# Norms and rope of queries and keys by pairs of heads inside the attention, and the context's attention in two halves behind it

## The chip, the core and the metric

The kernel runs on one core of one Trainium2 chip. The core has five engines that run at the same time and meet only at semaphores: TensorE (PE, matrix products and transposes by the identity), VectorE (DVE), ScalarE (ACT), GpSimd (POOL) and SyncE (SP, which issues transfers). The metric is the device time of one execution in microseconds.

## What is computed

One inference step of a trunk of two layers. Each layer has three mixers side by side (a state-space scan A, an attention B, a gated mixing C), one output projection, and a convolutional feed-forward. 512 latent tokens and 128 context tokens go through it together. The change touches B alone:

```python
def mla_queries(c_q, p, rope):
    q = (rmsnorm(c_q, p['q_a_norm']) @ p['w_uq']).reshape(bn, L, MLA_HEADS, MLA_QK)
    q = rmsnorm(q, p['q_norm'])            # per head, 96 channels
    if rope is not None:                   # latent tokens only
        q = concatenate([q[..., :64], apply_rope(q[..., 64:], *rope)])
    return q

# keys: 64 channels from the compressed kv, 32 shared rope channels, the same norm and rope
# latent queries see 128 cached context keys and the 512 latent keys;
# context queries see the 128 context keys alone, without rope
def one_block(q_blk):
    s = jnp.einsum('bqhd,bkhd->bhqk', q_blk, k).astype(F32) * ATTN_SCALE
    w = jax.nn.softmax(s, axis=-1).astype(v.dtype)
    return jnp.einsum('bhqk,bkhd->bqhd', w, v)
```

There are eight heads of 96 channels, with values of 64. All is in 32-bit floats.

## The kernel before

**Products.** Large products are made of two-part operands (a high part and the rest), each as three matmuls; the score product of one head and one key tile is such a three (`s`, L1267 to L1269). Small ones and transposes (L147) run on plain 32-bit operands.

**What sets the order.** The kernel is written in Tile with a scheduler that simulates the engines in time and gives each engine its own order. The written order is a wish: an instruction stands on its engine where the scheduler put it, and each engine then works strictly in that order. Buffers come from pools with a number of copies per name; a tile that is asked for waits until the oldest copy is free.

**The modulation as filler.** Each layer needs eight blocks of a product with w_mod, in 32 loads of 512 KB. A generator (`fill`) issues one load on SP's queue (L257) and its two matmuls (`mod`, L261) at each call; after a block come a copy on ScalarE (`modev`, L267), four transposes (`modt`) and a small reduce and add on VectorE (L240, L245). The loads have three buffers (`raw`). The calls are strewn over the projections and the attention, and what is left runs out at the end of the attention.

**Norms, before.** The query projection leaves `qs` (128 tokens of a tile on the partitions, 5 tiles, 8 heads, 96 channels; tile 4 is the context), the key projection `ks` (6 tiles: the cached ones and the latents, tile 5 the context). ScalarE squares each tile as it comes (`hsq`, L1061), VectorE sums the squares of each head (`ms`, L1062). `head_scales` turns sums into reciprocal roots in a chain of small operations on VectorE (L102 to L111, L1151 to L1157). `key_norms` writes the rope channels of all keys in one operation (L1163) and scales the others tile by tile (L1166). `query_norms` runs twice: for tile 4 alone, so that the context can start, and then for the four latent tiles: four scalings (L1174) and a rope of six operations over all heads (L1184 to L1189).

**Attention, before.** It begins with the context's: transposes of all eight heads (`ctr`), raw scores for the maxima (`cmx`, L1313), maxima of each query (`nm`, L1314), their transposition into extra rows of the queries (`nmt`, L1319), scores (`cs`, L1328), the exponentials (`Pc`, L1330) and weighted sums with row sums (`co`, L1341 and L1343). In between stand `turn` and `maxima` of heads 0 and 1. `turn(h)` transposes one head's queries and keys (`qt`, `kt`) and splits them into parts (`qh`, `ql`, `kh`, `kl`); `maxima(h)` makes raw scores in halves (`mx`, L1248) and reduces them (`nml`, L1250), with one call of `fill` at each of its four steps; `max_row(h)` transposes the negated maxima into row 96 of `qh` (`nmt`). Then a loop over four pairs of heads: `scores` of both heads (ten P tiles of 128x512, exponentials on ScalarE, L1271), `weighted` (VectorE sums of the P tiles, weighted sums `o`, L1287), and `turn`, `maxima` and `max_row` of the next pair's heads. Behind pairs 1 and 3 four heads are divided by their sums and squared for the norm ahead of the output projection (`wo`).

## Time and profile before

| | us |
|---|---|
| time, median of 3 runs | 1830.92 (1827.31 to 1836.54) |
| the profiled execution | 1831.83 |
| its span, first to last instruction | 1830.0 |
| TensorE busy | 1708.6 (93%) |
| VectorE busy | 1158.5 (63%) |
| ScalarE busy | 681.7 (37%) |
| GpSimd busy | 311.4 (17%) |
| TensorE clock granted, mean | 0.961 of full speed |

Layer 0's attention lies at about 241 to 382 us of the span, layer 1's at 1118 to 1265. The profile lists for each engine its busy time and the instructions in any window; for each wait what ended it; and for each instruction its start and length. PEclk is the share of full speed that TensorE's clock was granted in the window; full speed is 2.4 GHz. Matmuls overlap in the pipeline, so the distance between two starts tells their cost, not one's length. A plain 32-bit matmul leaves two records in the trace (the eight of `cmx` are listed as x16).

### The profile page before, as it was taken

Reading aid. Unit: us, or ns where it says so; the run is one execution under the profiler, and the core shown is the slowest. Engines: PE = TensorE matmul, PEld = TensorE weight load, DVE = VectorE, ACT = ScalarE, POOL = GpSimd, SP = SyncE. Lnnn points to the kernel's source line nnn. Section 1 sums busy time; section 2 is a strip of 40 time slices with the busy share of each in tenths; the row PEclk is TensorE's granted clock in tenths of the full one; section 3 lists DMA queues with packets and bytes.
Section 4 is the critical chain, followed back from the end, with each engine's and each line's share of the span. In section 5 each row is a group of like instructions: output and inputs, shape, how many; then the busy total and the mean of one; then the engine's idle time right before and its main releaser. Section 6 shows DMA issues by size and latency. Waiting matters only on the chain.

```text
span 1830.0 us, 28203 instructions
## 1 busy us (share of the span) xinstructions
PE 1708.6 (93%) x10864; PEld 1499.7 (82%) x10864; DVE 1158.5 (63%) x2421; ACT 681.7 (37%) x1210; POOL 311.4 (17%) x738
## 2 busy tenths in 40 slices
PE   6869789998999999999999888999989999999998
PEld 2668644478889999999999785445989999999998
DVE  6887875667664546456566668475786464555554
ACT  4334444433442424224244355353344232332241
POOL 2886200000195060540000210000000000000000
PEclk8989799999999999999999888999989999999999
DMA  9265453301453523223122633430222131221221
GB/s 297 70 177 152 113 166 122 105 24 47 129 160 111 152 55 117 76 81 110 47 78 79 169 87 121 157 127 1 70 70 93 35 104 47 92 89 39 81 82 58
DMA packets 192998, 182.44 MB, mean 100 GB/s; under 512 B 33438, under 2 KB 153052, under 8 KB 192864
## 3 DMA queue, kind: packets, MB, share of 16 engines
q1 hardware_dynamic: 170160, 154.33, 27.5%
q0 software_dynamic: 8272, 23.87, 4.4%
q10 hardware_dynamic: 14432, 2.44, 0.7%
q8 instruction: 86, 1.41, 0.3%
q14 instruction: 48, 0.39, 0.1%
HBM read 161.94 MB, written 18.64 MB: 99 GB/s over the span
## 4 chain that ended last, share of the span: by engine, by line
PE 75%; DVE 10%; DMA 8%; ACT 4%; issue 2%; POOL 1%; ACTq 1%; DVEq 0%; POOLq 0%
PE up L141 11%; PE up L143 11%; PE up L142 10%; PE dn L142 5%; PE dn L143 5%; PE dn L141 5%; PE mod L261 3%; DMA raw<-w_mod 3%; PE o L1287 3%; PE wo L141 1%; PE wo L143 1%; PE wo L142 1%; DVE wlo L118 1%; DMA raw<-ffn_w_up 1%; PE s L1267 1%
## 5 line engine op out<-in xcount | busy, mean ns | idle before, releaser
L141 PE MATMUL up<-hh,whi 128*128 128x322 f32 x1408 | 436.8, 315 | 9.8 <-ACT hh L357 8.9
L142 PE MATMUL up<-hl,whi 128*128 128x322 f32 x1408 | 439.2, 313 | 1.8 <-DVE hl L358 1.8
L143 PE MATMUL up<-hh,wlo 128*128 128x322 f32 x1408 | 439.8, 314 | 0.0
L141 PEld LDWEIGHTS up<-hh,whi 128*128 128x128 f32 x1408 | 266.1, 190 | 21.8 <-issue 10.8
L142 PEld LDWEIGHTS up<-hl,whi 128*128 128x128 f32 x1408 | 268.3, 191 | 2.7 <-DVE hl L358 2.7
L143 PEld LDWEIGHTS up<-hh,wlo 128*128 128x128 f32 x1408 | 267.3, 190 | 1.0 <-issue 1.0
L118 DVE TENSOR_TENSOR wlo<-raw,whi 128x1024 fp32r<-128x1024 f32 (+1 forms) x116 | 147.4, 1272 | 155.2 <-ACT whi L117 146.5
L142 PE MATMUL dn<-glo,dh 128*128 128x322 f32 (+1 forms) x704 | 217.7, 311 | 0.0
L143 PE MATMUL dn<-gh,dl 128*128 128x322 f32 (+1 forms) x704 | 217.4, 310 | 0.0
L141 PE MATMUL dn<-gh,dh 128*128 128x322 f32 (+1 forms) x704 | 208.9, 310 | 2.3 <-DVE xT L1501 1.5
L1501 DVE SCALAR_TENSOR_TENSOR xT<-dn,mod,xT 128x320 f32<-128x320 f32 (+2 forms) x288 | 112.1, 435 | 128.2 <-PE dn L143 128.1
L117 ACT CAST whi<-raw 128x1024 fp32r<-128x1024 f32 (+1 forms) x116 | 120.6, 1041 | 157.1 <-PE up L142 63.8
L1532 ACT ACTIVATE cv<-up,prm,cw 128x321 f32<-128x321 f32 x88 | 54.1, 619 | 259.0 <-PE up L143 255.0
L143 PEld LDWEIGHTS dn<-gh,dl 128*128 128x128 f32 x704 | 132.9, 189 | 0.0
L141 PEld LDWEIGHTS dn<-gh,dh 128*128 128x128 f32 x704 | 130.4, 189 | 2.8 <-DVE xT L1501 1.8
L142 PEld LDWEIGHTS dn<-glo,dh 128*128 128x128 f32 x704 | 132.7, 188 | 0.0
L261 PE MATMUL mod<-raw,sT 128*32 128x512 f32 x384 | 89.7, 642 | 21.7 <-DMA raw<-w_mod 19.8
L1533 DVE SCALAR_TENSOR_TENSOR cv<-up,cw,cv 128x320 f32<-128x320 f32 x88 | 48.3, 549 | 74.3 <-ACT cv L1532 74.1
L118 DVE TENSOR_TENSOR dl<-raw,dh 128x1024 fp32r<-128x1024 f32 x44 | 53.9, 1224 | 38.3 <-ACT dh L117 38.2
L1250 DVE TENSOR_REDUCE nml<-mx 128x1 f32<-128x640 f32 x64 | 51.1, 819 | 28.3 <-PE mx L1248 28.2
L117 ACT CAST dh<-raw 128x1024 fp32r<-128x1024 f32 x44 | 46.1, 1048 | 50.7 <-DMA raw<-ffn_w_down 44.5
L141 PE MATMUL wo<-yh,whi 128*128 128x322 f32 (+1 forms) x192 | 60.0, 318 | 1.7 <-ACT yh L117 0.9
(472 smaller groups left out, 3367.4 us busy)
## 6 DMA issues: line engine op xcount, KB each, us to landing
raw<-w_mod SPq DMA_DIRECT2D x96, 512.0 KB, 4.3
raw<-ffn_w_up SPq DMA_DIRECT2D x88, 512.0 KB, 3.9
raw<-ffn_w_down SPq DMA_DIRECT2D x44, 512.0 KB, 3.4
raw<-w_in SPq DMA_DIRECT2D x10, 512.0 KB, 5.0
we<-WEd POOLq DMA_DIRECT2D x8, 512.0 KB, 4.4
qt<-Qd POOLq DMA_DIRECT2D x8, 512.0 KB, 5.0
raw<-w_out SPq DMA_DIRECT2D x16, 256.0 KB, 4.8
raw<-w_out SPq DMA_DIRECT2D x8, 512.0 KB, 3.4
```

Source lines behind the costliest of these rows:

```text
L117: self.nc.scalar.copy(hi, raw)
L118: self.nc.vector.tensor_tensor(lo, raw, hi.bitcast(F32), op=OP.subtract)
L141: mm(ps, wh, xh, start=start, stop=False)
L142: mm(ps, wh, xl, start=False, stop=False)
L143: mm(ps, wl, xh, start=False, stop=stop)
L261: nc.tensor.matmul(ps[c:c + 32, :], self.sT[:, k, :], rv[:, j, :], start=k < 4, stop=k >= 4)
L1250: V.tensor_reduce(nm[:, tt:tt + 1], pb[:, :, :320], axis=AX.XY, op=OP.max, negate=True)
L1267: mm(ps, kh[i][:, kc_], qh[i], start=True, stop=False)
L1287: mm(pb[i * 64:(i + 1) * 64, 0], Vt[:, kt, 2 * p + i], Ps[i][kt], start=kt == 0, stop=kt == 4)
L1501: self.nc.vector.scalar_tensor_tensor(self.xT[:, m, a:b], po[:, a - lo:b - lo], self.modcol(l, gi, m, c), self.xT[:, m, a:b], op0=OP.mult, ...
L1532: A.activation(z[:, 0:321], po[:, 0:321], AF.Identity, bias=b, scale=c1)
L1533: V.scalar_tensor_tensor(z[:, 1:321], po[:, 0:320], c0, z[:, 1:321], op0=OP.mult, op1=OP.add)
```

## The change

Queries and keys keep their raw projections until the attention. The reciprocal roots are made ahead of it for all tiles at once, one chain of 40 columns for the queries and one of 48 for the keys. `prepare(p)` then scales and ropes the two heads of pair p: four kinds of operations over all tiles of these heads, and a rope of six. The written order puts `prepare(p + 1)` behind the scores of pair p's first head. `ready(h)` is `turn`, `maxima` with `fill`, and `max_row` of one head; the first two heads' stand ahead of the loop, a later pair's first head behind the first scores of the pair before, and its second behind the weighted sums. The context's attention goes from the front into the loop: `context(0)` (four heads) behind pair 1 and `context(1)` behind pair 2, each with its own transposes, maxima, scores and sums, its tiles out of the ten P buffers (three for each half), and its one-hot rows loaded anew in each half.

```diff
-        self.key_norms(pt, ks, sc, ms, krn, kg)
+        RK, RsK = self.head_scales(pt, keep, ms, sc, 5, 6, krn)
...
-            if tt == 4:
-                self.query_norms(l, pt, qs, sc, ms, tab, [4])
-        self.query_norms(l, pt, qs, sc, ms, tab, [0, 1, 2, 3])
+        RsQ, = self.head_scales(pt, keep, ms, sc, 0, 5)
...
+        def prepare(p):
+            hs = slice(2 * p, 2 * p + 2)
+            V.tensor_tensor(ks[:, :, hs, 0:64], ks[:, :, hs, 0:64],
+                            bc(RsK[:, :, hs, None], [128, 6, 2, 64]), op=OP.mult)
+            V.tensor_tensor(ks[:, :, hs, 64:96], bc(kg[:, :, None, :], [128, 6, 2, 32]),
+                            bc(RK[:, :, hs, None], [128, 6, 2, 32]), op=OP.mult)
+            V.tensor_tensor(qs[:, :, hs, :], qs[:, :, hs, :],
+                            bc(RsQ[:, :, hs, None], [128, 5, 2, 96]), op=OP.mult)
+            V.tensor_tensor(qs[:, 4, hs, 64:96], qs[:, 4, hs, 64:96],
+                            bc(self.qgr[l][:, None, :], [128, 2, 32]), op=OP.mult)
+            x1, x2 = qs[:, 0:4, hs, 64:80], qs[:, 0:4, hs, 80:96]
+            sh = [128, 4, 2, 16]
+            x = [at.tile(sh, F32, name=self.uid("qx"), tag=f"qx{i}") for i in range(4)]
+            tb = [bc(tab[:, i][:, :, None, :], sh) for i in range(4)]
+            for i, y in enumerate((x1, x2, x2, x1)):
+                V.tensor_tensor(x[i], y, tb[i], op=OP.mult)
+            V.tensor_tensor(x1, x[0], x[1], op=OP.subtract)
+            V.tensor_tensor(x2, x[2], x[3], op=OP.add)
...
+        def context(b):
+
+            qc, kc, Pc = (t("P", [128, 512], bufs=10).rearrange("p (h c) -> p h c", h=4)
+                          for _ in range(3))
...
+            A.copy(qc[96:100], bc(ps[:4, None, :128], [4, 4, 128]))
...
+        def ready(h):
+            turn(h)
+            for _ in maxima(h):
+                next(fill, None)
+            max_row(h)
+
+        prepare(0)
+        ready(0)
+        ready(1)
         merge_ac_stats()
         for p in range(4):
...
-            heads = (2 * p + 2, 2 * p + 3) if p < 3 else ()
-            out = weighted(p, [scores(2 * p), scores(2 * p + 1)])
-            for h in heads:
-                turn(h)
+            Ps = [scores(2 * p)]
+            if p < 3:
+                prepare(p + 1)
+                ready(2 * p + 2)
+            Ps.append(scores(2 * p + 1))
+            out = weighted(p, Ps)
             next(out)
-            for h in heads:
-                for _ in maxima(h):
-                    next(fill, None)
+            if p < 3:
+                ready(2 * p + 3)
             next(out)
-            for h in heads:
-                max_row(h)
+            if p in (1, 2):
+                context(p - 1)
```

How the scheduler's order changes is seen at three places. On TensorE in layer 1, right behind the query projection and two blocks of the modulation, there stood before:

```order
L147 MATMUL kt_11603<-ident,ks_11224 96x128 x5
L147 MATMUL kt_11633<-ident,ks_11224 96x128 x5
L147 MATMUL ctr_11572<-ident,qs_11223 96x128 x4
L147 MATMUL ctr_11578<-ident,qs_11223 96x128 x4
L147 MATMUL ctr_11584<-ident,ks_11224 96x128 x4
L147 MATMUL ctr_11590<-ident,ks_11224 96x128 x4
L1313 MATMUL cmx_11614<-kc_11570,qc_11569 128x128 x4
L1313 MATMUL cmx_11620<-kc_11570,qc_11569 128x128 x4
L147 MATMUL nmt_11643<-ident,nm_11613 8x128
L1328 MATMUL cs_11690<-qc_11569,kc_11570 128x128 x4
L1328 MATMUL cs_11697<-qc_11569,kc_11570 128x128 x4
L147 MATMUL qt_11596<-ident,qs_11223 96x128 x4
```

and stands now:

```order
L147 MATMUL kt_11560<-ident,ks_11237 96x128 x5
L147 MATMUL qt_11553<-ident,qs_11236 96x128 x4
L261 MATMUL mod_11601<-raw_11602,sT 32x512 x2
L261 MATMUL mod_11601<-raw_11642,sT 32x512 x2
L261 MATMUL mod_11601<-raw_11650,sT 32x512 x2
L1250 MATMUL mx_11571<-kh_1761_11527,qh_1757_11523 128x320 x2
L1250 MATMUL mx_11579<-kh_1761_11527,qh_1757_11523 128x320 x2
L147 MATMUL modt_11606<-ident,modev_11595 128x128 x4
L261 MATMUL mod_11601<-raw_11658,sT 32x512 x2
L1250 MATMUL mx_11587<-kh_1761_11527,qh_1757_11523 128x320 x2
L147 MATMUL nmt_11614<-ident,nml_11570 1x128
L1250 MATMUL mx_11597<-kh_1761_11527,qh_1757_11523 128x320 x2
```

The context's transposes, maxima and scores (`ctr`, `cmx`, `nmt`, `cs`) are gone from between the first head's keys and queries, only head 0 is transposed before the first maxima, and three loads' `mod` matmuls stand between.

On VectorE in layer 1, from the latent tiles' reciprocal roots (`Rs`) to the last step of the rope, there stood before:

```order
L1157 TENSOR_TENSOR Rs_1738_11494<-rs_y_1737_11484,sc_10013 128x32
L1174 TENSOR_TENSOR qs_11223<-qs_11223,Rs_1738_11494 128x768 x4
L1314 TENSOR_REDUCE nm_11613<-cmx_11614 128x4
L1314 TENSOR_REDUCE nm_11613<-cmx_11620 128x4
L1184 TENSOR_TENSOR qx_11500<-qs_11223,qtab_11243 128x512
L1185 TENSOR_TENSOR qx_11501<-qs_11223,qtab_11243 128x512
L1186 TENSOR_TENSOR qx_11502<-qs_11223,qtab_11243 128x512
L1187 TENSOR_TENSOR qx_11503<-qs_11223,qtab_11243 128x512
L1188 TENSOR_TENSOR qs_11223<-qx_11500,qx_11501 128x32x16
L1189 TENSOR_TENSOR qs_11223<-qx_11502,qx_11503 128x32x16
```

Now there stand, from the roots of all five tiles to the first operation of the second pair's rope:

```order
L1165 TENSOR_TENSOR Rs_1744_11479<-rs_y_1743_11469,sc_10026 128x40
L1178 TENSOR_TENSOR qs_11236<-qs_11236,Rs_1744_11479 128x5x192 x4
L1180 TENSOR_TENSOR qs_11236<-qs_11236,q_normr_1991 128x2x32
L1187 TENSOR_TENSOR qx_11543<-qs_11236,qtab_11256 128x128
L1187 TENSOR_TENSOR qx_11544<-qs_11236,qtab_11256 128x128
L1187 TENSOR_TENSOR qx_11545<-qs_11236,qtab_11256 128x128
L1187 TENSOR_TENSOR qx_11546<-qs_11236,qtab_11256 128x128
L1180 TENSOR_TENSOR qs_11236<-qs_11236,q_normr_1991 128x2x32 x3
L1188 TENSOR_TENSOR qs_11236<-qx_11543,qx_11544 128x4x2x16
L1189 TENSOR_TENSOR qs_11236<-qx_11545,qx_11546 128x4x2x16
L1187 TENSOR_TENSOR qx_11754<-qs_11236,qtab_11256 128x128
L1187 TENSOR_TENSOR qx_11755<-qs_11236,qtab_11256 128x128
```

and from the last product of the third pair's rope on, to the first maxima:

```order
L1187 TENSOR_TENSOR qx_11991<-qs_11236,qtab_11256 128x128
L1232 SCALAR_TENSOR_TENSOR ql_1759_11525<-qt_11553,qg_1983,qh_1757_11523 96x512
L1188 TENSOR_TENSOR qs_11236<-qx_11988,qx_11989 128x4x2x16
L1189 TENSOR_TENSOR qs_11236<-qx_11990,qx_11991 128x4x2x16
L1187 TENSOR_TENSOR qx_12288<-qs_11236,qtab_11256 128x128
L1187 TENSOR_TENSOR qx_12289<-qs_11236,qtab_11256 128x128
L1187 TENSOR_TENSOR qx_12290<-qs_11236,qtab_11256 128x128
L1187 TENSOR_TENSOR qx_12291<-qs_11236,qtab_11256 128x128
L1188 TENSOR_TENSOR qs_11236<-qx_12288,qx_12289 128x4x2x16
L1189 TENSOR_TENSOR qs_11236<-qx_12290,qx_12291 128x4x2x16
L1252 TENSOR_REDUCE nml_11570<-mx_11571 128x1
```

All four pairs' scalings (x4) stand together ahead of the first rope, and all four ropes ahead of the first maxima (L1252); nothing of `prepare(1)` to `prepare(3)` stands behind the first scores. Layer 0 has the ropes of pairs 1 to 3 among the first head's four maxima.

On ScalarE in layer 0, around the end of the second pair, there stood before (`yB` and `S` are the weighted sums and row sums of a pair, `P` the exponentials):

```order
L1229 ACTIVATE qh_489_2950<-qt_3303,qg_333 96x512
L1208 COPY yB_2944<-o_3330 128x512
L1211 COPY S_2948<-o_3330 64x512
L267 COPY modev_3410<-mod_3372 128x512
L267 COPY modev_3586<-mod_3416 128x512
L1259 CAST qh_488_2949<-nmt_3434 1x512
L1271 ACTIVATE P_3450<-s_3446 128x512
L1271 ACTIVATE P_3456<-s_3452 128x512
L1271 ACTIVATE P_3462<-s_3458 128x512
L1236 ACTIVATE kh_492_2953<-kt_3513,kg_336 96x512
```

and stand now, with the first half of the context (`P_3572` and `P_3573` are its queries and keys, `P_3574` its exponentials, `whi` the high part of a w_out weight):

```order
L1309 ACTIVATE P_3573<-ctr_3582,kg_336 96x512
L1238 ACTIVATE kh_484_2912<-kt_3508,kg_336 96x128
L267 COPY modev_3724<-mod_3549 128x512
L117 CAST whi_3939<-raw_3938 128x1024
L117 CAST whi_4167<-raw_4166 128x1024
L1318 COPY P_3572<-cnmt_3595 4x512
L1322 ACTIVATE P_3574<-cs_3598 128x512
L1273 ACTIVATE P_3642<-s_3638 128x512
L1273 ACTIVATE P_3648<-s_3644 128x512
L1273 ACTIVATE P_3654<-s_3650 128x512
```

Two casts of w_out weights now stand ahead of the copy of the context's maxima, and behind it stand the exponentials of the context and of the next head.

## Rows read from the trace of the kernel before

**Rows 1.** Page, busy us, share of span, instructions of one engine
```profile
PE 1708.6 (93%) x10864; PEld 1499.7 (82%) x10864; DVE 1158.5 (63%) x2421; ACT 681.7 (37%) x1210; POOL 311.4 (17%) x738
```

**Rows 2.** Windows of A and B: span, busy us by engine, PEclk, DMA share, GB/s
```profile
241.30:275.30 34.00, 29.59 (x171) 13.94 (x170) 21.79 (x40) 14.34 (x29) 3.27 (x6) 0.95 0.71 231
275.30:382.30 107.00, 100.71 (x473) 51.73 (x471) 68.13 (x122) 50.31 (x98) 0.24 (x2) 0.97 0.30 95
1118.30:1156.10 37.80, 29.19 (x154) 17.98 (x152) 24.88 (x52) 14.54 (x28) 0.00 (x0) 0.82 0.34 110
1156.10:1264.90 108.80, 102.24 (x473) 51.90 (x470) 68.23 (x122) 50.63 (x97) 0.24 (x2) 0.97 0.30 97
```

**Rows 3.** Waits of TensorE, 1118 to 1156 us: for whom, total, times, longest
```profile
PE nmt L147 <- DVE nm L1314: 2.1, 1, 2.1
PE ctr L147 <- DVE qs L1177: 1.6, 1, 1.6
```

**Rows 4.** Windows inside layer 1's A, the same columns
```profile
1127.00:1133.00 6.00, 2.77 (x18) 2.28 (x17) 6.00 (x9) 1.49 (x3) 0.00 (x0) 0.78 0.01 3
1133.00:1140.00 7.00, 7.00 (x38) 5.78 (x40) 4.48 (x9) 4.99 (x9) 0.00 (x0) 0.63 0.00 0
...
1148.00:1156.10 8.10, 8.10 (x49) 3.45 (x47) 2.05 (x4) 1.94 (x7) 0.00 (x0) 0.97 0.49 151
```

**Rows 5.** Waits of TensorE, 241 to 276 us
```profile
PE mod L261 <- DMA raw<-w_mod: 4.2, 4, 3.2
```

**Rows 6.** DMA issues, 241 to 276 us: count, KB each, median to landing
```profile
raw<-w_mod SPq DMA_DIRECT2D x15, 512.0 KB, 4.9
```

**Rows 7.** Timeline of VectorE, layer 1: start, us, line, operation, count
```profile
1122.50 0.41 DVE L1177 TENSOR_TENSOR qs<-qs,q_normr 128x256 f32<-128x256 f32 x1
1122.83 0.18 DVE L1151 TENSOR_TENSOR ms<-ms,sc 128x32 f32<-128x32 f32 x1
...
1126.39 0.19 DVE L1157 TENSOR_TENSOR Rs<-rs_y,sc 128x32 f32<-128x32 f32 x1
1126.62 3.56 DVE L1174 TENSOR_TENSOR qs<-qs,Rs 128x768 f32<-128x768 f32 x4
...
1131.30 0.68 DVE L1184 TENSOR_TENSOR qx<-qs,qtab 128x512 f32<-128x512 f32 x1
1131.89 0.68 DVE L1185 TENSOR_TENSOR qx<-qs,qtab 128x512 f32<-128x512 f32 x1
...
1134.42 0.68 DVE L1189 TENSOR_TENSOR qs<-qx,qx 128x512 f32<-128x512 f32 x1
```

**Rows 8.** Groups of TensorE, 241.3 to 282 us: busy us, mean ns
```profile
L1313 PE MATMUL cmx<-kc,qc 96*128 96x128 f32 x16 | 2.2, 281 | 0.0
L1328 PE MATMUL cs<-qc,kc 104*128 104x128 f32 x16 | 1.9, 275 | 0.0
...
L147 PE MATMUL ctr<-ident,ks 128*96 128x128 f32 x8 | 1.2, 278 | 0.0
```

**Rows 9.** Timeline of TensorE before layer 1's first score
```profile
1149.49 0.43 PE L1341 MATMUL co<-Pc,Vt 128*64 128x128 f32 x2
1149.85 0.41 PE L1343 MATMUL co<-Pc,ones 128*32 128x128 f32 x2
1150.19 0.43 PE L1341 MATMUL co<-Pc,Vt 128*64 128x128 f32 x2
```

**Rows 10.** Waits of TensorE, 276 to 383 us
```profile
PE mod L261 <- DMA raw<-w_mod: 3.2, 2, 2.2
...
PE mx L1248 <- DVE nml L1250: 0.5, 1, 0.5
```

**Rows 11.** Waits of TensorE, 1156 to 1265 us
```profile
PE mod L261 <- DMA raw<-w_mod: 3.6, 2, 1.9
PE mx L1248 <- DVE nml L1250: 0.8, 2, 0.5
```

**Rows 12.** Window inside layer 0's B, columns as in the windows above
```profile
335.00:342.00 7.00, 6.75 (x24) 4.39 (x21) 5.42 (x7) 3.74 (x5) 0.00 (x0) 0.58 0.66 218
```

More of the change, by code (lines that the diff above doesn't have):

```diff
@@ L1191, in attention @@
-    def attention(self, l, M, yb, at, es, qs, ks, Vt, yB, yA, yc, ssc, fill):
+        def prepare(p):
[16 more added lines that the diff above has]
+            V.tensor_tensor(x2, x[2], x[3], op=OP.add)
@@ L1194, in attention @@
+        return prepare
+    def attention(self, l, M, yb, at, prepare, qs, ks, Vt, yB, yA, yc, ssc, fill):
         nc, V, A = self.nc, self.nc.vector, self.nc.scalar
@@ L1347, in attention @@
-        at2 = es.enter_context(self.tc.tile_pool(name=f"at2{l}", bufs=1, side=self.sides[1]))
+        def context(b):
+            qc, kc, Pc = (t("P", [128, 512], bufs=10).rearrange("p (h c) -> p h c", h=4)
+                          for _ in range(3))
+            hs = slice(4 * b, 4 * b + 4)
+            nc.sync.dma_start(out=kc[96:100].rearrange("p h c -> p (h c)"),
+                              in_=self.I["k_onehot"][hs, b * 512:(b + 1) * 512])
+            for src, dst, g in ((qs[:, 4], qc, qg), (ks[:, 5], kc, kg)):
+                ps = self.pa("ctr")
+                for i in range(4):
+                    self.tr(ps[:96, i * 128:(i + 1) * 128], src[:, 4 * b + i, :])
+                A.activation(dst[:96].rearrange("p h c -> p (h c)"), ps[:96], AF.Copy, scale=g)
+            nm = t("cnm", [128, 4], bufs=2)
+            ps = self.pa("cmx")
+            for i in range(4):
+                mm(ps[:, i * 128:(i + 1) * 128], qc[:96, i], kc[:96, i], start=True, stop=True)
+            V.tensor_reduce(nm, ps.rearrange("p (h c) -> p h c", h=4), axis=AX.X, op=OP.max,
+                            negate=True)
+            ps = self.pa("cnmt")
+            self.tr(ps[:4, :128], nm)
+            A.copy(qc[96:100], bc(ps[:4, None, :128], [4, 4, 128]))
+            ps = self.pa("cs")
+            for i in range(4):
+                mm(ps[:, i * 128:(i + 1) * 128], kc[:100, i], qc[:100, i], start=True, stop=True)
+            A.activation(Pc.rearrange("p h c -> p (h c)"), ps, AF.Exp, scale=SCALE)
+            for p in range(2 * b, 2 * b + 2):
+                po = self.pb("co")
+                for i in range(2):
+                    Ph = Pc[:, (2 * p + i) % 4]
+                    mm(po[i * 64:(i + 1) * 64, 0, :128], Vt[:, 5, 2 * p + i], Ph,
+                       start=True, stop=True)
+                    r = (2 * p + i) % 4 * 32
+                    mm(po[r:r + 32, 1, :128], self.ones[:, :32], Ph, start=True, stop=True)
+                put(p, po[:, 0], po[:, 1], 128, CX)
+            V.reciprocal(S[:, b, 512:640], S[:, b, 512:640])
```

105 lines of the change are left out of this document (19 added, 86 removed).

## The prediction

> **What bounds the kernel now.** The busy shares of the page say that TensorE is the bound nearly everywhere (93% of the span) [rows 1]. The change touches only the attention of the two layers, so the reader should look at four stretches [rows 2]. I call **A** the stretch in which queries and keys are normed and the context's attention runs: from layer 0's first w_mod matmul at 241.3 us, and from layer 1's last query projection at 1118.3 us, to the first score matmul (275.3 and 1156.1). **B** is the rest, up to the first matmul of the output projection (382.3 and 1264.9). A lasts 34.0 and 37.8 us, B 107.0 and 108.8. TensorE is busy for 29.6 of the 34.0 us and 29.2 of the 37.8 in A, 100.7 and 102.2 in B [rows 2]. So B has some 6.5 us of idle TensorE in each layer, and A more, but a busy microsecond of A isn't a microsecond at full speed: the granted clock of layer 1's A is 0.82 against 0.97 in B [rows 2].
>
> What ends last in A differs by layer. In layer 1 the waits of TensorE end on VectorE's work, 2.1 us on the maxima of the context's scores and 1.6 us on the first scaled queries [rows 3], and in 1127 to 1133 us VectorE is busy for all of the 6.0 us while TensorE does 2.8 [rows 4]. In layer 0 they end on the w_mod transfers, 4.2 us in four waits [rows 5]; there the DMA engines are busy 0.71 of the time [rows 2], and one 512 KB load takes 4.9 us from issue to landing [rows 6], with three `raw` buffers for them. So A of layer 1 is set by a chain on VectorE, A of layer 0 by a stream of transfers, and B by TensorE.
>
> **VectorE's operations.** The cost of one piece by its size: 128x512 operations of the rope start 0.59 us apart (1131.30, 1131.89), the 128x256 one takes its engine for 0.33 us (1122.50 to 1122.83), four of 128x768 take 3.56 us [rows 7]. Between these lie 0.06 us an instruction and 1.05 ns an element, so a 128x128 piece is worth 0.20 us, and one of 128x960 1.07 us. No row shows a 128x128 operation with these strides, so I bound it by 0.18 us (the small operations' own duration, 1122.83) and 0.33 us (128x256) [rows 7]. The rope of all pairs goes from six operations of 0.6 us to 24 of 0.2 and a bit: 3.8 us to about 5.0 (4.3 to 7.9 between the bounds). The scaling of the queries stays at about 4.7 us in four pieces for five, the key norms at about 5.3 in eight for seven. One of two chains of reciprocal roots is saved (14 small operations, about 2.4 us by 0.17 us each), but that chain for tile 4 ran beside the projection, so nothing of it is on the path, and the one that is left now has to wait for all five tiles.
>
> **How much is really "by pairs".** The order of VectorE answers this: all four scalings (and all key norms) stand together ahead of the first pair's rope, and the ropes of the other three pairs stand ahead of the first head's maxima. Only the rope of pairs 1 to 3 is out of the way of the first transposes, and it is in the way of the maxima behind them (18 operations, 3.75 us).
>
> **A of layer 1.** The last two squares now stand behind a copy of the modulation on ScalarE and come 1 to 3 us later; from there the chain of roots takes 14 steps of about 0.23 us (1126.39 to 1126.62 [rows 7]) with 1.8 us of other work between, the scalings 4.3, the first rope 1.7: the first pair's queries are ready at about 1133, where the whole rope ended at 1135.1 [rows 7]. Transposes (1.0 us), three w_mod loads that stand ahead of the maxima on TensorE (3 to 4 us, they cover the 3.75 us of ropes), four maxima of 0.8 us each and the max row follow: first score at about 1143.5. That is 12.6 us earlier; A would be 25.2 us.
>
> **A of layer 0.** By the order 13 w_mod loads stand ahead of the first score, two fewer than now. Three lie in buffers; the others come in at three in each 4.3 to 4.9 us of transfer plus 1.0 us of matmul, so 1.8 to 2.0 us apiece. First of these landed at about 246.6, the tenth 16 to 18 us later: first score at about 264.5, 10.8 us earlier. Transfers set this, and the change doesn't make them faster. The bounds are 0 (the buffers' cycle is the limit throughout) and 13.
>
> **What B takes over.** The context's matmuls come into B: transposes 2.4 us (two of 1.2), maxima 2.2, scores 1.9 [rows 8], and eight half pairs of weighted sums at 0.70 (0.36 and 0.34: 1149.49, 1149.85, 1150.19 [rows 9]), 5.6; with the overlapping ends off, about 11.3. One pair of sums (1.4) lies behind the first score already, so 9.9. With them go one head's maxima (1.2) and 0.5 of small transposes: 11.6 us for layer 1. In layer 0 two w_mod loads more, 2.0: 13.6. B is bound by TensorE, so this work costs its full time there except where it fills an idle place.
>
> What it can fill: the w_mod waits of 3.2 and 3.6 us [rows 10, 11], of which I take half (1.9), since the scheduler has something to put there only where the halves happen to stand; and the waits on the maxima, listed with 0.5 and 0.8 [rows 10, 11] and with the shorter gaps beside them about 1.5. What it adds: the context's own chain (maxima, reduce, transpose, copy, scores) is three hand-overs long, and in the second half its links follow one another on TensorE with nothing between: 1.7 us (the same chain waited 2.1 us at one link in A [rows 3]). In the first half two casts of w_out stand ahead of the copy that this chain waits for on ScalarE, and behind it stand the exponentials of the next head; their weights come late: 2 us. The bounds of these two together are 0 and 8, if the cast waits for a whole load (4.9 [rows 6]). Three tiles of each half come out of the ten `P` buffers: the fourth and fifth score matmuls of a head then wait for the head before; I give this nothing in the middle and 1 us a layer at the top. Fill and new waits: −3.4 + 3.7, about +0.3 a layer.
>
> **The clock.** In layer 1's A the granted clock falls to 0.78 and then to 0.63 after 6 us in which TensorE was busy for 2.8 [rows 4]; in B of layer 0 it was 0.58 for seven microseconds right behind a wait for w_mod of 2.2 us [rows 10, 12]. The change takes the context's matmuls, TensorE's cover, out of just this stretch. The Trainium skill, "TensorE: Matmul & The Clock Gate", section "What's actually happening" says that the throttled state is the default, and activity lifts it. That speaks against the change, and the trace agrees as far as it goes (0.63 behind a thin stretch [rows 4]); by that page the thinner stretch would throttle longer than it does now, which is the slower rival below. In the sum I take no extra loss, since the three loads, maxima and transposes ahead of the first score make TensorE busy again.
>
> **Sum.** Layer 0: −10.8 + 13.6 + 0.3 = +3.1. Layer 1: −12.6 + 11.6 + 0.3 = −0.7. Together +2.4, on the profiled run's own 1831.83 us (its span of 1830.0 and 1.83 around it): 1834.2, or 1834. That run is 0.9 us above the median of 1830.92, far less than anything here decides. Nothing outside A and B moves by more than a microsecond.
>
> **Rivals.**
> *Faster: the context fills B's holes.* For it: B has 6.3 and 6.6 us of idle TensorE [rows 2], more than half of it waits for w_mod, and the stretch at 0.58 costs another 2.8 us (7 us at 0.58 where 0.97 is usual [rows 12]). If independent work stands at each of these, 6.7 us a layer are won and the new waits don't come: 1831.8 + 1.8 − 13.4 = about 1820. Against it: the rows show two w_mod waits in each B, at fixed places, and the halves stand after the second and third pairs only. Chance 0.20.
> *Slower: the clock.* One mechanism, at the end of A: TensorE with half the work for 10 us and more stays at a low clock into the first score phase. If 15 us of each layer run at 0.6 for 0.97, that is 15 x 0.38 = 5.7 us a layer: 1834.2 + 11.4 = about 1846. It decides from about 8 us a layer on (6 us in all, 1840). For it: 0.63 and 0.58 in the rows named; against it: the clock is back at 0.97 over 1148 to 1156 and over all of B, which has few gaps [rows 2]. Chance 0.27, with all of what the chain over ScalarE can add.
> *It doesn't do what it says.* If the first pair's preparation isn't earlier at all (the order has it behind all scalings), A of layer 1 ends 2 to 3 us later than I say; that is inside the forecast.
>
> **How the numbers follow.** The forecast, a change of at most 0.5% (9 us, about what a measurement of this kernel can tell from no change), has 0.53; the faster rival 0.20, the slower one 0.27. Range: the likeliest case is 1826 to 1842 by the bounds named; 0.8 of the chance needs most of both rivals, 1818 to 1848.
>
> **What would show it.** In the profile after: first scores near 264.5 and 1143.5; B 13 to 14 us longer in layer 0 and 11 to 12 in layer 1; the waits of B on w_mod at 1 to 3 us; a wait of the context's score matmul on ScalarE's copy in layer 0; VectorE fully busy up to about 1137. Wrong would be: a B that grows by less than 8 us (the holes were filled), or a granted clock under 0.8 over the first pair's scores (the clock).

## Result: the changed kernel is 0.7% slower

The changed kernel takes 1847.42 us (median of 7 runs, 1842.78 to 1852.44), the kernel before 1836.53 in the same comparison (7 runs, 1827.31 to 1836.81). The ratio is 1.0074 with a 95% interval of 1.0052 to 1.0096: some 13.6 us (it is the ratio of the means; the medians differ by 10.9). The forecast was 1834 and no change; the time lies inside the range of 1818 to 1848, on its slower side.

The profiled execution is the one of 1847.42 us, with a span of 1845.6 us. TensorE is busy for 8 us less than before [rows 1] in a span that is 15.6 us longer:

```profile
PE 1700.2 (92%) x10866; PEld 1496.7 (81%) x10866; DVE 1159.0 (63%) x2433; ACT 687.6 (37%) x1212; POOL 312.6 (17%) x740
```

The four stretches, to be held against [rows 2]. A of layer 0 runs from the first w_mod matmul to the first score, A of layer 1 from the last query projection; columns as there:

```profile
243.46:273.25 29.79, 21.06 (x87) 6.63 (x86) 16.79 (x50) 7.43 (x14) 3.28 (x6) 0.83 0.67 211
273.25:394.70 121.45, 111.55 (x570) 62.30 (x568) 73.30 (x131) 60.02 (x112) 0.24 (x2) 0.97 0.31 96
1128.70:1159.90 31.20, 14.14 (x77) 5.98 (x74) 22.50 (x64) 9.56 (x17) 3.36 (x6) 0.73 0.39 128
1159.90:1282.30 122.40, 112.83 (x561) 62.73 (x559) 73.42 (x131) 59.66 (x112) 0.24 (x2) 0.94 0.29 95
```

So B grew from 107.0 to 121.4 us and from 108.8 to 122.4, by 14.4 and 13.6. Of this TensorE's busy time is 10.8 and 10.6, and its idle time (span less busy) 3.6 and 3.0: it was 6.3 and 6.6 us before and is 9.9 and 9.6 now. A of layer 0 shrank from 34.0 to 29.8 us only. A of layer 1 is 31.2 us; from the last query projection (it ends at 1115.6 us) to the first score (1156.1) it was 40.5 before, so it gave back 9.3. (What starts at 1118.3, where the prediction begins A of layer 1, is not the last query projection but the first transposes of keys behind it.)

A of layer 0 on TensorE's timeline (start, length, line, operation, count, and in brackets the idle time before and what ended it):

```profile
237.03 6.50 PE L824 MATMUL glu<-gl,wg 128*128 128x320 f32 x12 [3.00 <-ACT gl L819]
243.46 1.91 PE L261 MATMUL mod<-raw,sT 128*32 128x512 f32 x12
248.59 1.05 PE L261 MATMUL mod<-raw,sT 128*32 128x512 f32 x4 [3.21 <-DMA raw<-w_mod]
...
256.27 1.05 PE L261 MATMUL mod<-raw,sT 128*32 128x512 f32 x4 [0.93 <-DMA raw<-w_mod]
...
261.01 1.92 PE L261 MATMUL mod<-raw,sT 128*32 128x512 f32 x4 [2.90 <-DMA raw<-w_mod]
```

and its wait on the loads, beside the 4.2 us of [rows 5]:

```profile
PE mod L261 <- DMA raw<-w_mod: 7.0, 3, 3.2
```

TensorE does three loads at once, sits 3.2 us until the fourth lands, and waits again at each turn. Six `glu` matmuls (twelve records) ahead of it took 6.5 us where the kernel with only the context moved (below) did them in 4.1. The granted clock of this A is 0.83 against 0.95 before.

In layer 1 TensorE waits 13.3 us for the first pair's queries:

```profile
PE qt L147 <- DVE qs L1189: 13.3, 1, 13.3
```

VectorE there (start, length, line, operation, count):

```profile
1140.30 0.20 DVE L1165 TENSOR_TENSOR Rs<-rs_y,sc 128x40 f32<-128x40 f32 x1
1140.53 4.37 DVE L1178 TENSOR_TENSOR qs<-qs,Rs 128x960 f32<-128x960 f32 x4
...
1144.95 0.89 DVE L1187 TENSOR_TENSOR qx<-qs,qtab 128x128 f32<-128x128 f32 x4
...
1146.37 0.28 DVE L1189 TENSOR_TENSOR qs<-qx,qx 128x128 f32<-128x128 f32 x1
...
1150.91 0.28 DVE L1189 TENSOR_TENSOR qs<-qx,qx 128x128 f32<-128x128 f32 x1
```

The scalings of all pairs take 4.4 us, the first pair's rope ends at 1146.65 (`qs<-qx,qx` at 1146.37), the last pair's at 1151.2. Four 128x128 products take 0.89 us, 0.22 each, where 0.20 was taken. In B of layer 0 the waits [rows 10] have other names now:

```profile
PE cs L1321 <- ACT P L1318: 3.1, 2, 2.4
PE mx L1250 <- ACT kh L1238: 2.8, 4, 1.0
PE mod L261 <- DMA raw<-w_mod: 2.1, 3, 0.9
```

### The profile page after: what moved, and what is told of

It is laid out like the page before. It is cut to its first block, busy times and chain, and to the rows that moved or that the text cites. A ratio compares the mean times of both kernels' runs of the same rounds, so it can differ in the third digit from the quotient of the medians.

```text
span 1845.6 us, 28207 instructions
## 1 busy us (share of the span) xinstructions
PE 1700.2 (92%) x10866; PEld 1496.7 (81%) x10866; DVE 1159.0 (63%) x2433; ACT 687.6 (37%) x1212; POOL 312.6 (17%) x740
## 4 chain that ended last, share of the span: by engine, by line
PE 73%; DVE 11%; DMA 7%; ACT 4%; issue 2%; POOL 1%; ACTq 1%; SPq 0%; DVEq 0%; POOLq 0%
PE up L141 11%; PE up L143 10%; PE up L142 10%; PE dn L142 5%; PE dn L143 5%; PE dn L141 5%; PE mod L261 3%; PE o L1289 2%; DMA raw<-w_mod 2%; DMA raw<-ffn_w_up 1%; PE wo L141 1%; PE wo L142 1%; PE wo L143 1%; DVE wlo L118 1%; PE s L1269 1%
## 5 line engine op out<-in xcount | busy, mean ns | idle before, releaser
L118 DVE TENSOR_TENSOR wlo<-raw,whi 128x1024 fp32r<-128x1024 f32 (+1 forms) x116 | 146.6, 1265 | 155.6 <-ACT whi L117 149.6
L117 ACT CAST whi<-raw 128x1024 fp32r<-128x1024 f32 (+1 forms) x116 | 120.7, 1042 | 158.1 <-PE up L142 58.9
L118 DVE TENSOR_TENSOR dl<-raw,dh 128x1024 fp32r<-128x1024 f32 x44 | 54.0, 1227 | 40.6 <-ACT dh L117 40.5
L1252 DVE TENSOR_REDUCE nml<-mx 128x1 f32<-128x640 f32 x64 | 51.5, 820 | 28.8 <-PE mx L1250 28.7
L1273 ACT ACTIVATE P<-s 128x512 f32<-128x512 f32 x80 | 47.8, 597 | 44.0 <-PE s L1271 41.9
```

The costliest lines, as they stand in the source:

```text
L117: self.nc.scalar.copy(hi, raw)
L118: self.nc.vector.tensor_tensor(lo, raw, hi.bitcast(F32), op=OP.subtract)
L1252: V.tensor_reduce(nm[:, tt:tt + 1], pb[:, :, :320], axis=AX.XY, op=OP.max, negate=True)
L1273: A.activation(P, ps, AF.Exp, scale=SCALE)
```

## Experiments: which part of the change costs

The change has three parts that can be undone one by one: the context's halves behind, the norms by pairs, and a loop that readies one head at a time (`ready`) where the loop before readied two together. The kernels below are all compositions of these. "A" in the table runs, in both layers, from the end of the last query projection to the first score, B from there to the first output projection matmul, read from the starts in each profiled execution; the ratio is that of the times. One execution's stretches carry some 5 us of chance: the code ahead of the first attention, the same in all of these kernels, took 174.6 to 180.0 us.

| kernel | context | norms | loop | ratio (95%) | A0 | B0 | A1 | B1 |
|---|---|---|---|---|---|---|---|---|
| before | front | all heads | two heads | 1 | 42.8 | 107.0 | 40.5 | 108.8 |
| e1 | behind | all heads | two heads | 1.0002 (0.9982 to 1.0022) | 38.7 | 117.1 | 33.9 | 116.0 |
| e6 | behind | pairs | two heads | 1.0015 (0.9990 to 1.0041) | 38.8 | 120.1 | 36.4 | 118.2 |
| e5 | behind | all heads | one head | 1.0089 (1.0062 to 1.0116) | 40.6 | 122.3 | 28.7 | 121.1 |
| changed | behind | pairs | one head | 1.0074 (1.0052 to 1.0096) | 41.4 | 121.4 | 31.2 | 122.5 |
| e9 | behind | pairs | two at first, then one | 1.0049 (1.0030 to 1.0069) | 42.7 | 116.4 | 37.0 | 117.4 |
| e10 | behind | pairs | one at first, then two | 1.0070 (1.0045 to 1.0095) | 37.1 | 122.7 | 28.8 | 120.7 |
| e2 | front | pairs | one head | 1.0188 (1.0160 to 1.0217) | 57.2 | 105.3 | 54.0 | 106.5 |

**e1, the context behind alone.** In the kernel before:

```diff
-        with self.tc.tile_pool(name=f"actx{l}", bufs=1, side=self.sides[1]) as cx:
...
+            if p in (1, 2):
+                context(p - 1)
```

> The kernel before, its norms over all heads and its loop untouched, with the context's attention in two halves behind pairs 1 and 2 (that half of the change alone). Theory one, cover: in front the context's 11 us of TensorE work per layer lay beside the w_mod loads (layer 0) and VectorE's chain (layer 1); 15 loads stand ahead of layer 0's first score here as before, so its stretch A stays at 34 us or a little under, layer 1's falls from 37.8 to about 31, and B grows by 12 to 14 us in each layer: 1845 to 1852. Theory two, the clock: the same, with a granted clock under 0.8 in A of layer 0 too, and most of the loss ahead of the first score. Theory three, the norms by pairs are at fault: within 4 us of the kernel before.

It costs nothing. Theories one and two fall, and with them the picture that the context in front was covered. Theory three has the time, but e6 below acquits the norms. In the profiled execution B takes over 10.1 and 7.2 us (9.9 of the context's 11.3 were not in B before) and A gives back 4.1 and 6.6. The context fills no idle places in B: TensorE's idle time there is 8.4 and 8.6 us, for 6.3 and 6.6 before. Three windows of it (B of layer 0, A and B of layer 1):

```profile
274.40:391.60 117.20, 108.79 (x549) 58.56 (x547) 69.63 (x125) 57.89 (x112) 0.24 (x2) 0.99 0.29 95
1122.60:1156.60 34.00, 18.76 (x87) 8.27 (x85) 23.84 (x55) 9.61 (x17) 3.28 (x6) 0.75 0.44 143
1156.60:1272.60 116.00, 107.44 (x552) 58.22 (x550) 71.27 (x127) 57.45 (x111) 0.24 (x2) 1.00 0.29 93
```

**e2, the context in front, the rest as changed.**

```diff
-        prepare(0)
+        for p in range(4):
+            prepare(p)
+        for b in range(2):
+            context(b)
         ready(0)
         ready(1)
```

> The changed kernel with both halves of the context's attention written ahead of the first head again, all pairs' preparation ahead of them (the norms by pairs and the new loop alone). Theory one, cover: A of layer 0 with its 15 loads back at 34 us, B back at 107 to 109: 1829 to 1836. Theory two, the clock: the same time, since TensorE is as busy in A as before, with a granted clock of 0.9 or more in A of layer 0. Theory three, the norms by pairs: 1842 or more.

Far outside all of these but theory three's "or more": 34 us slower. With norms by pairs there is no early start for the context's queries any more; the wait of TensorE on them in layer 1 is

```profile
PE ctr L147 <- DVE qs L1180: 13.7, 1, 13.7
```

where it was 1.6 us [rows 3]. So the norms by pairs need the context behind, but that doesn't say that they cost anything there. (e2 has the new loop too, which is priced below.)

**e3 and e4, no context at all,** in the kernel before and in the changed one:

```diff
+        V.memset(yB[:, :, CX:], 0.0)
+        V.memset(S[:, :, 512:640], 1.0)
```

> The kernel before with the context's attention left out (its columns are constants). It prices the context in front. Theory one, cover: in layer 0 next to nothing is won beyond the pair of sums in B (1.4 us), since 15 loads at 34.0/15 = 2.27 us each still stand ahead of the first score; in layer 1 some 5 to 8 us of 37.8: 1821 to 1826. If nothing covers it in front, 2 x 11.3 us are won: about 1809.

> The changed kernel with the context's attention left out (its columns are constants). It prices the context behind. Theory one, cover: B loses all of the context's work and its waits (11.3 and about 2 us in each layer), 25 us less than the changed kernel: 1818 to 1824, as fast as the kernel before without its context. Theory two, the clock in A: A is as thin as in the changed kernel, so A keeps 29.8 and 31 us and the kernel stays 5 us or more slower than the kernel before without its context.

e3 is at 0.9885 (0.9856 to 0.9914), e4 at 0.9898 (0.9861 to 0.9934). The context in front costs 21 us for some 22.6 us of TensorE work, so it was hardly covered at all; behind, in the changed kernel, it costs 32 (1.0074 less 0.9898). The expectation of theory one for e3 was wrong, and the one without cover (22.6 us) came. That for e4 was right by the number, though the cover from which it argues isn't there.

**e5 and e6, norms and loop apart.** e5 has the norms of before with the new loop, e6 the reverse:

```diff
-            Ps = [scores(2 * p)]
-            if p < 3:
-                prepare(p + 1)
-                ready(2 * p + 2)
-            Ps.append(scores(2 * p + 1))
...
+            out = weighted(p, [scores(2 * p), scores(2 * p + 1)])
+            if p < 3:
+                prepare(p + 1)
+            for h in heads:
+                turn(h)
```

> The changed kernel with the norms and the rope of the kernel before (all heads at once, ahead of the attention); the loop that readies one head at a time and the two halves of the context stay. Known by now: the halves behind, with norms and loop of before, cost nothing (1.0002). Theory one, the loop by single heads is at fault: about 13 us slower than the kernel before, 1.005 to 1.009. Theory two, the norms by pairs are at fault: no difference from the kernel before, 0.998 to 1.002. Theory three, each has its share: 1.002 to 1.005.

> The changed kernel with the loop of the kernel before (both heads' scores, then both heads turned, their maxima and max rows); norms by pairs and the halves of the context stay. Theory one, the loop by single heads is at fault: no difference from the kernel before, 0.998 to 1.002. Theory two, the norms by pairs are at fault: 1.005 to 1.009. Theory three, each has its share: 1.002 to 1.005.

Theory one, clearly: the loop by single heads is at fault, by 16 us with the norms of before (e5 against e1) and 11 with those by pairs (changed against e6). In e6:

```profile
276.40:396.50 120.10, 110.98 (x543) 59.98 (x541) 69.70 (x125) 57.37 (x112) 0.24 (x2) 0.96 0.28 91
1127.60:1164.00 36.40, 19.69 (x95) 9.56 (x93) 25.47 (x70) 9.84 (x17) 3.36 (x6) 0.72 0.41 129
1164.00:1282.20 118.20, 109.23 (x544) 59.90 (x541) 69.95 (x125) 57.19 (x112) 0.24 (x2) 0.97 0.29 92
```

A of layer 1 has a granted clock of 0.75 in e1 and 0.72 in e6, as low as the changed kernel's 0.73, and these two are not slower. The norms by pairs make no difference that these times can tell (e6 against e1, the changed kernel against e5). They don't make the first queries ready earlier: in e5 the whole rope of layer 1 ends 15.7 us behind the last query projection (1148.65 from 1132.98),

```profile
1147.96 0.69 DVE L1189 TENSOR_TENSOR qs<-qx,qx 128x512 f32<-128x512 f32 x1
```

in the changed kernel the first pair's alone after 17.95 (1146.65 from 1128.70).

**e9 and e10, the two places of the loop.** e9 readies the first two heads as before, e10 the later ones:

```diff
-        ready(0)
-        ready(1)
+        for h in range(2):
+            turn(h)
+        for h in range(2):
+            for _ in maxima(h):
+                next(fill, None)
+        for h in range(2):
+            max_row(h)
```

> The changed kernel in which only the first two heads are readied as before the change (both turned, both heads' maxima, both max rows), so that 15 loads and both heads' maxima stand ahead of layer 0's first score again (13 and one head's in the changed kernel); inside the loop it stays as changed. Theory front: the changed loop costs through what it shifts from A, where TensorE waits for loads or VectorE, into B, where TensorE is the bound; then this kernel has lost it: 0.999 to 1.003. Theory inside: the cost is made in the loop, where one head at a time is readied between two score phases (waits of the raw scores on the copy of the keys, 2.8 us in layer 0's B): 1.006 or more.

> The other half: the first two heads are readied one after the other as in the changed kernel (13 loads and one head's maxima ahead of layer 0's first score), and inside the loop both heads are readied together, behind both heads' scores, as before the change. Theory front: 1.006 or more. Theory inside: 0.999 to 1.003. If both kernels lie at 1.003 to 1.005, each half costs its part.

Neither theory alone. The new front costs 10 us by itself (e10 against e6), as theory front had it for e10; e9 lies between the two theories, and whether the inside costs anything by itself isn't settled (e9 against e6: the intervals overlap). Over whole profiled executions TensorE is idle (span less busy) for 144.9 to 145.8 us in the three kernels with one head ready at the first score (e5, changed, e10) and for 139.1 to 140.2 in the three with two (e1, e6, e9): 5 to 6 us go with the front. The table shows what the front does: with one head ready at the first score, the three kernels' B are 120.7 to 122.7 us, with two ready 116.0 to 120.1. In layer 1 A gives that back (28.7 to 31.2 against 33.9 to 37.0), in layer 0 it doesn't (37.1 to 41.4 against 38.7 to 42.7), though two w_mod loads and seven of the maxima's matmuls have left it. (In layer 1 A holds nine loads in the kernel before, e1, e6 and e9, eight in the changed one, seven in e5 and six in e10; the loads that e5 and e10 lack against the changed kernel stand ahead of A, in the projections, which in e10 take 41.9 us from the end of the input projection for 35.7.)

**e7 and e8, small loads:** 64 KB in place of 512 KB for each w_mod load, in the kernel before and the changed one.

```diff
-                nc.sync.dma_start(out=rv, in_=src[:, 2 * kp:2 * kp + 2])
+                    nc.sync.dma_start(out=rv[:, 0, 0:128], in_=src[:, 2 * kp, 0:128])
```

> The kernel before with 64 KB in place of 512 KB for each load of w_mod (a piece of it that the matmuls read over and over). It prices the stream of transfers in the kernel before. The waits on w_mod listed for A and B sum to 4.2 + 3.2 + 1.3 + 3.6 = 12 us: 0.990 to 0.995. Both theories expect it; it is the measure for the next.

> The changed kernel with the same small loads. Theory one, transfers: A of layer 0 is a stream of loads at 2.3 us each whatever else stands there, so the changed kernel gains more from small loads than the kernel before, 20 us or more (7.0 + 2.1 + 1.5 + 2.5 of listed waits and what they do to the clock), and ends within 4 us of the kernel before with small loads. Theory two, the loss is VectorE's and ScalarE's (norms or loop): it stays 10 to 15 us above the kernel before with small loads.

e7 is at 1.0015 (0.9992 to 1.0039): making the loads small won none of the 12 us of listed waits. With other loads the scheduler made another order, and B of layer 1 is 113.6 us with a new wait in the place of the old ones:

```profile
PE s L1271 <- ACT qh L1263: 3.9, 2, 3.6
```

e8 is at 1.0029 (1.0004 to 1.0054), 8 us less than the changed kernel, where theory one wanted 20 or more, and level with e7. That the loss needs the loads, as theory one says, is a hint only, since the order changed in e7.

**e11 and e12, no filler in the attention,** in the changed kernel and in e6. The last eight blocks of the modulation are left out with loads and matmuls:

```diff
+        if len(blocks) == 8:
+            nc_.vector.memset(self.mod[l][:, 16:48, :], 1.0)
+            for _ in range(33):
+                yield
+            return
```

> The changed kernel without the last eight modulation blocks of each layer (32 loads of w_mod and their matmuls in each layer are left out, constants stand in their place), so that nothing but the attention's own work stands between its steps. To be read against e12, the same with the loop of before. Theory front: the loop costs because it lengthens the stream of loads' share in B and leaves A waiting for it; without loads it costs nothing, the two lie within 0.003 of each other. Theory inside: readying one head at a time exposes hand-overs between the engines (keys' copy to raw scores to maxima to the max row), with fewer fillers more than now: this kernel is 0.004 to 0.010 slower than e12. Both some 50 us under the kernel before (0.965 to 0.98).

> The kernel e6 (norms by pairs, context in halves behind, the loop of before) without the last eight modulation blocks of each layer, as e11. Theory front: within 0.003 of e11. Theory inside: 0.004 to 0.010 faster than e11.

e11 is at 0.9759 (0.9735 to 0.9784), e12 at 0.9841 (0.9818 to 0.9863). Both theories miss: without the filler the new loop is 15 us *faster*. B of both layers, first e11, then e12:

```profile
264.00:362.75 98.75, 92.13 (x467) 55.79 (x467) 68.30 (x117) 55.64 (x106) 0.24 (x2) 1.00 0.00 1
1124.00:1225.80 101.80, 95.20 (x467) 58.42 (x467) 68.50 (x117) 55.51 (x106) 0.24 (x2) 0.97 0.00 1
```

```profile
270.90:378.95 108.05, 99.20 (x453) 57.92 (x453) 67.70 (x112) 51.97 (x104) 0.24 (x2) 0.91 0.00 1
1139.85:1246.80 106.95, 98.00 (x450) 57.86 (x448) 67.16 (x110) 51.85 (x104) 0.24 (x2) 0.92 0.00 1
```

The new loop's B is 9.3 and 5.2 us shorter. Waits are the smaller part of it: TensorE's idle time is 6.6 us in either B of e11 and 8.9 and 9.0 in e12, so 2.2 and 2.4 us. The rest is busy time, at a granted clock of 1.00 and 0.97 in e11 and of 0.91 and 0.92 in e12. Over the whole executions it is plainer, first e11, then e12:

```profile
PE 1639.8 (92%) x10546; PEld 1485.2 (83%) x10546; DVE 1152.0 (64%) x2399; ACT 676.7 (38%) x1196; POOL 310.5 (17%) x740
PE 1657.9 (92%) x10546; PEld 1491.8 (83%) x10546; DVE 1155.4 (64%) x2399; ACT 672.2 (37%) x1196; POOL 311.5 (17%) x740
```

The same 10546 records keep TensorE busy for 18 us longer in e12, while it is idle for 150.4 us in e11 (span 1790.2) and 149.4 in e12 (1807.3). The mean granted clock is 0.948 to 0.957 in all runs of e11 and 0.944 to 0.948 in all of e12. In layer 0's B of e12 it is at its lower level (0.50) for 10 us from 320.0 on; that begins within the longest of these waits, which ends at 321.2:

```profile
PE cnmt L147 <- DVE cnm L1320: 3.0, 1, 3.0
PE o L1295 <- DVE kl L1245: 1.9, 1, 1.9
PE mx L1256 <- DVE nml L1258: 1.7, 4, 0.5
```

What does the filler cost? By the times the 64 loads of both layers cost 58 us in the new loop (1.0074 less 0.9759, of 1836) and 32 us in the old one (1.0015 less 0.9841), each give or take 6. By the stretches it is the same: in B of layer 0, 19 loads cost 22.7 us (121.4 less 98.7) in the changed kernel, 17 loads 12.1 us (120.1 less 108.0) in e6; in layer 1, 18 loads 20.6 and 17 loads 11.2. One load is 1.05 us of TensorE where it stands alone. The filler doesn't go into the old loop's waits: idle TensorE is 9.1 and 9.0 us in e6 with it, 8.9 and 9.0 in e12 without. In the new loop it adds 3.3 and 3.0 us of idle time. The rest of the difference is busy time, 19.4 us for the 19 loads and 11.8 for the 17 in layer 0, and goes with the granted clock: with the filler it rises from 0.91 to 0.96 in the old loop and falls from 1.00 to 0.97 in the new one (layer 1: from 0.92 to 0.97, and from 0.97 to 0.94). An estimate from these shares: B's length times what the share lacks of 1 falls by about 5 us in the old loop of layer 0 and rises by about 3.6 in the new one, some 8 of the 10.6 us by which the two prices differ. Why the clock moves so isn't shown.

**e13 to e16, the filler called earlier.** The thought behind these was that the filler costs its full time only where no idle places are, and should be called elsewhere. They call it in the steps of the key and query projections, 11 times (e13) or 17 times (e14) in the changed kernel, 17 in the kernel before (e15) and in e5 (e16); the edit for 17:

```diff
         for kt in range(6):
+            for _ in range(2):
+                next(fill, None)
...
         for tt in (4, 0, 1, 2, 3):
+            for _ in range(1):
+                next(fill, None)
```

> The changed kernel with 11 calls of the filler moved into the key and query projections (one in each of their steps), so that 9 or 10 loads stand in each B in place of 18 or 19. Theory place: each load taken out of B gives back its 1.1 us there (22.7 us for 19 loads by e11) and costs about half of that in the projections, where TensorE is idle a fifth of the time: 10 to 14 us less than the changed kernel, 0.998 to 1.003. Theory transfers: as many loads, the same time, 1.004 to 1.010.

> The changed kernel with 17 calls moved, so that one load is left in each B. Theory place: B near 100 to 104 us as without the filler, 20 us less in each layer, half of it given back in the projections and in A: 15 to 25 us less than the changed kernel, 0.993 to 1.0. Theory transfers: 1.004 or more.

> The kernel before with the same 17 calls moved. Theory place: its B has holes that the filler used for 4 of each 10 us, so less is won in B (some 10 us a layer) and as much is lost ahead of it: no gain, 0.998 to 1.006, and slower than the changed kernel with the 17 calls moved. Theory transfers: it moves as the changed kernel does.

> The changed loop and the context's halves with the norms of before, 17 calls moved. The whole rope of layer 1 was ready 15.7 us behind the last query projection with the norms of before (e5), the first pair's 17.9 us with the norms by pairs. So this should be as fast as e14 or 2 to 5 us faster: 0.991 to 0.999.

Measured: 1.0216 (1.0186 to 1.0246), 1.0302 (1.0270 to 1.0333), 1.0313 (1.0276 to 1.0350) and 1.0289 (1.0252 to 1.0326). Every range of theory place missed, e16's too, and theory transfers has only its open bound ("1.004 or more") for e14. B's length did as theory place says: 104.0 us in layer 0 of e14, 17.4 less than the changed kernel's with 18 loads fewer, and 104.8 in e15, only 2.2 less than the kernel before's with 16 fewer. But holes aren't the reason: e15's B is idle for 7.8 us (6.3 before), and its granted clock is 0.90 where it was 0.97. And the stretch from the end of the input projection to that of the query projection went from 56.5 us in the kernel before to 111.3 in e14. The two windows and the waits of TensorE in the first:

```profile
176.50:287.80 111.30, 75.56 (x378) 48.41 (x382) 54.76 (x130) 33.42 (x60) 13.10 (x42) 0.75 0.46 137
316.80:420.80 104.00, 97.55 (x478) 58.78 (x475) 70.81 (x121) 56.28 (x107) 0.23 (x2) 0.97 0.10 31
```

```profile
PE glu L824 <- ACT gl L819: 14.1, 2, 11.4
PE mod L261 <- DMA raw<-w_mod: 8.9, 7, 3.4
```

The loads stand in front of the projections' steps on TensorE and are waited for, 8.9 us; `glu` waits 14.1 us for ScalarE, where the kernel before has no such wait in this stretch. How the one leads to the other wasn't followed up. Called so, the filler costs more there than in B, and no kernel of the study that does the whole work beats the one before; e1 equals it.

## Why the prediction was wrong

**What held.** B's growth: 13.9 and 11.9 were forecast, 14.4 and 13.6 measured. In part that is luck: the forecast was 13.6 and 11.6 of work with 0.3 of waits, since new waits of 3.7 were to be offset by 3.4 of filled ones; the work took 10.8 and 10.6, the new idle time is 3.6 and 3.0, and nothing was filled. The waits named came: on w_mod 2.1 and 2.5 us in the two B, and of the context's scores on ScalarE's copy 3.1 in each. The order's reading that nothing is really by pairs held, as did the first pair's readiness (17.4 us behind the last query projection forecast, 1133 less 1115.6; 17.95 measured). VectorE's chain to it from the last sum of squares, 11.0 us by the terms, took 11.1 (from 1135.54); the 1 to 3 us by which the squares were to come later aren't in that sum, and didn't come. That the context's move alone costs nothing held by the time (e1).

**Step that failed first: "A of layer 0", the price of a load.** I took 1.8 to 2.0 us a load from a buffer's cycle and put the first score 10.8 us earlier. The rows to divide were at hand: 15 loads [rows 6] in 34.0 us [rows 2] are 2.27 us each. Thirteen are then 29.5 us; 29.8 were measured, from the first w_mod matmul on. That is 6.6 us of the miss. That the division comes out so well is luck too, for it is no constant of the chip: e1 did 15 in 29.1 us, 1.94 each, with a granted clock of 0.88 there, and e5, e6, e9 and e10 lie between, at 2.0 to 2.2. Another 2.8 us came ahead of A, where I had excluded any: the `glu` matmuls at half clock. It is one execution's; e10 and e4, with the same instructions ahead of the loads, had 10.2 and 8.8 us from the query projection to the end of `glu`, the changed kernel 11.7.

**In "A of layer 1"** the first score came 31.2 us behind the last query projection, where 27.9 was forecast (1143.5 less 1115.6). What was short is the stretch behind the first pair's queries, 10.5 us forecast and 13.2 measured: three w_mod loads were taken for it, and six stand there (1147.79 to 1159.46), one of them waited for, 1.3 us.

**Step that was missing: the loop.** The prediction priced the norms, the context and the clock. The loop by single heads stands in it only as "one head's maxima" and "two w_mod loads more" inside B's sum; it has no term of its own, and it is the part that costs (e5, e6). How it costs is shown in part only. Five to six us are idle TensorE that goes with the front (e9, e10). The listed waits of B, 9.6 against 8.9 us in layer 0, don't make the difference. A rival that nothing here separates is the clock: the mean granted clock over all runs is 0.958 in the changed kernel, 0.954 in e5 and e9 and 0.959 in e10, against 0.963 in e1 and 0.962 in e6. Each thousandth is 1.8 us of the time at most (less, as a low clock costs nothing while TensorE waits), so up to 8 us between the changed kernel and e6 and up to 16 between e5 and e1. Whether the loop lowers the clock, and by what, isn't shown.

**"Faster: the context fills B's holes"** came in no kernel. B's idle time grew in the changed kernel, and in e1 too; e1's B is short (10.1 and 7.2 us more than before) at a granted clock of 0.99 and 1.00 where 0.97 was usual.

**"Slower: the clock"** has the time, 1846, by luck; its mechanism didn't come. The clock fell in layer 1's A, to 0.50 for 11 us,

```profile
1137.00:1143.00 6.00, 0.00 (x0) 0.00 (x0) 5.76 (x18) 1.51 (x5) 2.42 (x5) 0.50 0.00 0
1143.00:1148.00 5.00, 1.20 (x8) 0.84 (x12) 4.96 (x19) 0.11 (x1) 0.00 (x0) 0.50 0.00 0
1148.00:1154.00 6.00, 4.67 (x22) 1.56 (x16) 4.81 (x16) 0.58 (x1) 0.00 (x0) 0.75 0.52 158
```

but over the first pair's scores, where it was to stay low, it was 1.00 in both layers (273 to 290 and 1160 to 1176 us), and over the whole of B 0.97 and 0.94. And e1 and e6 have nearly as thin an A of layer 1 and as low a clock there and lose nothing. The Trainium skill, "TensorE: Matmul & The Clock Gate", section "What's actually happening", says that the clock is throttled by default and that activity releases it; these rows agree (0.50 behind a stretch without a matmul). In this stretch the low clock could cost little, as TensorE waited for VectorE through most of it: it was busy for 1.2 of the first 11 us. Where TensorE has work, a low clock does cost (18 us of busy time between e11 and e12).

**The sum.** From the last query projection on, A and B of layer 0 together are 13.0 us longer than before, of layer 1 4.3; all else is 1.7 shorter. Forecast were 3.1 and −0.7. The miss of 13.2 (1847.4 for 1834.2) is then 6.6 of the loads and 2.8 ahead of them in layer 0, 3.3 in layer 1's A and 0.5 and 1.7 in the two B, less the 1.7.

**What stays open.** By the times the new loop costs 11 us over e6, by the profiled executions' A and B only 3 (316.5 against 313.5). The profiled execution of e6 is one of its slower ones (1844.98 at a median of 1840.98), which accounts for 4 of the 8. From the end of the input projection to the first output projection matmul, both layers together, the profiled executions take 409.4 us in the changed kernel, 409.5 in e6, 408.1 in e10, 399.0 in e1 and 391.3 before: they don't place the 11 us, and e6 and e1 differ by more in them than in time. The loop's cost may also need the context and the loads in B: without the context the changed kernel's norms and loop cost 2 us, give or take 9 (e4 against e3), with small loads 3, give or take 6 (e8 against e7). Where the cost arises, and how it divides between the front and the inside of the loop, isn't settled.

## What to carry to other kernels

Background work that a scheduler strews into another loop has no price of its own: here the same loads cost 0.5 us each in one loop and 0.9 in another. A rewrite may therefore win alone and lose with the filler in place; time it without the filler too. And before a shorter stretch is called one with fewer holes, divide it into idle and busy time and look at the granted clock: here the waits were the obvious reason and the smaller one. And take the price of a stream from its own stretch (so many transfers in so many us), not from one transfer's latency.

## What was not expected of the hardware

Two things. Transfers eight times smaller (64 KB for 512 KB) changed the time of the kernel before by 0.15%, less than its measurement tells, although 12 us of TensorE's waits were listed on them. And code that is the same in all kernels of the table, ahead of the first attention, took from 174.6 us (the changed kernel) to 180.0 (e10) up to the end of layer 0's input projection, at granted clocks that differ (0.91 and 0.88): single profiled executions don't tell differences of under 5 us.
